# Five edits to a two-layer decoder trunk: RWKV's logistic functions on ScalarE, the skip load, the order of the rotary tables, the norms' sums and one buffer

## The chip, the cores and the metric

The kernel runs on one core of one Trainium2 chip, in one launch. The metric is the device time of a run in microseconds (us), and what is compared is the median of several runs. All times inside a run are counted from the start of its profiled span.

## The reference

Two consecutive layers of a hybrid decoder trunk are computed for one sequence of 512 tokens, model width 1024, everything in float32. Cut to the parts that the change touches:

```python
def even_mixer(h, ...):                      # layer 0
    proj = rms_norm(h, norm) @ w_in
    y_mla = mla_group(...)                   # 8 heads, rotary positions, causal softmax
    y_rw = rwkv7_group(...)                  # 8 heads of 64
    return jnp.concatenate([y_mla, y_rw], axis=-1) @ w_out

def rwkv7_group(p, ...):
    w_log = -jax.nn.softplus(-(w0 + jnp.tanh(xw) @ w2)) - 0.5
    decay = jnp.exp(-jnp.exp(w_log.astype(jnp.float32)))
    a = jax.nn.sigmoid(a0 + xa @ a2)
    ...
    y = wkv7_scan(r_h, heads(decay), k_h, v_h, -kk, kk * a_h)
    ...

def mamba2_mixer(h, ...):                    # layer 1
    ...
    y = ssd_chunked(xf * dt[..., None], dt * A, b_in, c_in)
    y = y + xf * d_skip.astype(jnp.float32)[:, None]
    ...
```

The decay is exp of a constant times the logistic function of its argument, so each pair of heads needs two logistic functions of 128x512 elements: one for the decay, one for `a`. After each mixer come a cross-attention into 256 memory tokens and a SwiGLU feed-forward, each behind its own RMS norm and added into the residual.

## The kernel before, in words

Activations lie transposed: the residual `hT` is eight tiles of 128 features by 512 tokens. Every large product is made in three matmuls on reduced-precision halves. An operand is split into a high part (`whi`, `xh`: a copy with rounding on ScalarE, L122) and a low part (`wlo`, `xl`: the remainder, on VectorE or GpSimd, L136 and L139), and TensorE adds high by high, low by high and high by low into one PSUM bank named `lin` (all matmuls on L117). Weights arrive as blocks `wraw` of 128x1024 floats (512 KB) in two buffers (L175), requested by SyncE's queue; `lo_turns` says which engine makes the next `wlo`. A block's buffer is asked for again as soon as both halves of the block before have been made.

Stages, in us: first norm and projection 0 to 60; RWKV and MLA, interleaved, 60 to 460; cross-attention 0 from 465 to 555; feed-forward 0 to 914; the Mamba mixer to 1353; cross-attention 1 to 1426; feed-forward 1 to the end. A scheduler turns the written order into one list per engine, by its own simulation of times; each engine then works through its list in order, and waits where an operand is late. Around RWKV the written order comes from a `Dense` queue of projection pieces that `weave` mixes with the steps of RWKV's head pairs (`front`, `within`, `across`) and with MLA's pairs.

What the change touches:

- `prenorm` (L337 to L368) splits `hT` into `xh` and `xl` and sums the squares of the eight tiles into `ss`. Squares 0 to 2 (0 to 3 in the first norm) are made on GpSimd, the others on ScalarE. Additions below `DVA` (5; 6 in the first norm) are GpSimd's, the others VectorE's. `fin` puts one matmul with ones on `ss` (`preno_pr`) and two activations that make the reciprocal root `R`. There are six such norms; `SQA, DVA, PX` stand on L180.
- In the first norm each finished `lin` bank is scaled by `R` into a `pd` tile on VectorE before the bank can be filled again.
- `mla_setup` (L1222) makes the rotary tables: positions, range reduction (`rope`, `angk`, `nrk`: some twenty operations on VectorE) and sines on ScalarE. It is called on L814 behind the last operation in `switch`; the Mamba layer's small loads (`odpar`, `dcol`) are issued beside it from ScalarE's queue (L816 to L820). `dcol` holds the skip factor of the Mamba heads and is first read at about 1006 us (L139, `y<-xf,dcol,odd_m_py`).
- `front` (L936) begins a head pair. It calls `sigmoid` (L931) on the tiles `fa` (decay) and `av` (a): an exponential on ScalarE, then an addition of 1 (L933) and a reciprocal (L934) on VectorE. The running sum of `fa` (L952, `fb`) and two exponentials of it (`E`, `fc`) follow. There are four pairs, so eight such functions.
- `steps` (L1510) makes the Mamba step sizes. The exponentials `ecum` of the running sums (`cum`) take the buffer `z0`, and two DMAs carry them to DRAM; the gate `z` uses the same buffer next.

Of the kernel before, what the change touches and what calls it, by code (L numbers as in the profile page):

```python
# [10 lines left out]
F32 = mybir.dt.float32  # L11
# [4 lines left out]
ALU = mybir.AluOpType  # L16
# [63 lines left out]
def kernel(ctx: ExitStack, tc: tile.TileContext, a: dict, out: bass.AP, stage: str = "exfoXF"):  # L80
# [64 lines left out]
    def cst(k):  # L145
        o, n = _COFF[k]
        return ctab[:, o:o + n]

    ident = cst("ident")
    bones = cst("bones")  # L150
    invf = cst("invf")
    ones = cp.tile([P, P], F32, name="ones")
    V.memset(ones, 1.0)
# [25 lines left out]
    held = []  # L179
    SQA, DVA, PX = (3, 5, 3)  # L180
    HOLDK = 3
# [155 lines left out]
    def prenorm(xp, gains, tmp=("ss", "sq", 2), tag="ps", before=lambda k: None):  # L337
# [3 lines left out]
        tss, tsq, bufs = tmp  # L341
        ss = xp.tile([P, T], F32, tag=tss, name=nm("ss"))
        for k in range(KD):
            before(k)
# [6 lines left out]
            xl.append(l_)  # L351
            if k == 0:
                tt(G, ss, hT[k], hT[k], ALU.mult)
            else:
                sq = xp.tile([P, T], F32, tag=tsq, name=nm("sq"), bufs=bufs)
                if k < (4 if gains is evc else SQA):
                    tt(G, sq, hT[k], hT[k], ALU.mult)
                else:
                    act(sq, hT[k], AF.Square)
                tt(G if k < (6 if gains is evc else DVA) else V, ss, ss, sq, ALU.add)  # L360

# [378 lines left out]
    def even_mixer():  # L740
# [6 lines left out]
        with pool("rwkv", side="right") as rp, pool("mlac", side="right") as cp_, pool("rwdram", space=DRAM) as dp:  # L747
# [15 lines left out]
            with psum(lin=4, ps=2):  # L763
# [49 lines left out]
                turn_rows(rows, False)  # L813
                with tc.issue_after(switch[-1].ins):  # L814
                    mla_setup(ml, xp, rt)
                    nc.scalar.dma_start(odpar[96:128, 0:1], a["ssm_dt_bias"][0].rearrange("(p o) -> p o", o=1))  # L816
                    nc.scalar.dma_start(odpar[96:128, 1:2], a["ssm_a_log"][0].rearrange("(p o) -> p o", o=1))
                    dsrc = a["ssm_d"][0].rearrange("(i j) -> j i", j=2)
                    for j in range(2):
                        nc.scalar.dma_start(dcol[j * 64:(j + 1) * 64, :], dsrc[j].partition_broadcast(64))  # L820
                logs()
# [86 lines left out]
    def rwkv_steps(rp, rt, rw, loaded):  # L908
# [21 lines left out]

        def sigmoid(o, x, negb):  # L931
            act(o, x, AF.Exp, scale=-1.0, bias=negb)
            V.tensor_scalar(o, o, 1.0, None, op0=ALU.add)  # L933
            V.reciprocal(o, o)  # L934

# [544 lines left out]
    def odd_mixer():  # L1480
# [11 lines left out]
        with pool("odd") as op, pool("oddram", space=DRAM) as dp, \  # L1492
# [17 lines left out]
            def steps(o):  # L1510
# [17 lines left out]
                nc.sync.dma_start(cdram, cum[q, :])  # L1528
                ecum = i_("z0")
                act(ecum[q, :], cum[q, :], AF.Exp)  # L1530
# [280 lines left out]
```

## Time and profile before

| what | value |
|---|---|
| median of three runs | 1801.33 us (1799.94 to 1806.09) |
| profiled execution: its own time | 1798.9 us |
| profiled execution: span of the trace | 1797.1 us |
| mean granted TensorE clock | 0.981 |
| TensorE busy | 1733.4 us (96%) |
| VectorE busy | 1087.6 us (61%) |
| ScalarE busy | 742.9 us (41%) |
| GpSimd busy | 232.8 us (13%) |
| chain that ended last | PE 86%, DVE 6%, DMA 3%, ACT 3% |

PE is TensorE, DVE VectorE, ACT ScalarE, POOL GpSimd, SP SyncE; L12 is line 12 of the kernel printed above. A row of a timeline gives the start and the duration of an instruction (or of a run of equal ones, x7) and, in brackets, how long its engine sat idle before it and what ended that. [...] Matmuls are pipelined, so a busy TensorE is not one at its peak.

### The profile page before, as it was taken

What the parts mean: (1) busy time and instruction counts of PE and PEld (TensorE: products, weight loads), DVE (VectorE), ACT (ScalarE), POOL (GpSimd) and SP (SyncE); (2) the same over time, 40 slices, a digit from 0 to 9 for tenths busy, and PEclk for the clock granted to TensorE, in tenths of its full rate; (3) what the DMA queues carried; (4) which work ended last, traced back from release to release, by engine and by line L of the source; (5) the groups of instructions that cost most, each with busy time, mean ns of one, the idle gap of its engine ahead of it and who ended that gap; (6) DMA issues with size and microseconds to landing.
All of it is one profiled execution on the core that took longest, in us unless ns stands there. A gap on an engine that the chain in (4) does not pass through costs nothing.

```text
span 1797.1 us, 25503 instructions
## 1 busy us (share of the span) xinstructions
PE 1733.4 (96%) x10192; PEld 1379.4 (77%) x10192; DVE 1087.6 (61%) x1707; ACT 742.9 (41%) x1273; POOL 232.8 (13%) x204
## 2 busy tenths in 40 slices
PE   7899999999899999999998999999999999999998
PEld 5667767777677888888876777777887788888886
DVE  6585687758566434343467779787776844443533
ACT  3443455455344213222345555454545532222222
POOL 6222211212312000101020010100020200000000
PEclk9999999999899999999998999999999999999999
DMA  5232100012213333333333433333232133333232
GB/s 160 71 92 85 49 20 25 26 60 75 79 38 92 94 99 95 100 94 101 99 91 110 112 95 115 103 118 99 91 117 71 52 102 94 94 105 95 94 97 92
DMA packets 171869, 157.15 MB, mean 87 GB/s; under 512 B 12075, under 2 KB 150182, under 8 KB 171750
## 3 DMA queue, kind: packets, MB, share of 16 engines
q1 hardware_dynamic: 169574, 155.51, 28.8%
q8 instruction: 80, 1.31, 0.3%
q14 instruction: 39, 0.32, 0.1%
q10 hardware_dynamic: 2176, 0.01, 0.1%
HBM read 150.90 MB, written 4.59 MB: 87 GB/s over the span
## 4 chain that ended last, share of the span: by engine, by line
PE 86%; DVE 6%; DMA 3%; ACT 3%; issue 1%; SPq 1%; ACTq 0%; DVEq 0%
PE lin L117 67%; PE xattn_q L117 2%; PE odd_m_py L117 2%; PE rw_x L117 1%; PE mla_sc L117 1%; DMA wraw<-in_ev_w_in_dram 1%; DVE xl L139 1%; PE rw_gram L117 1%; PE mla_q L117 1%; PE mla_pv L117 1%; PE mla_kv L117 1%; PE rw_y L117 1%; DVE wlo L136 1%; PE xattn_po L117 1%; PE mla_pT L1447 1%
## 5 line engine op out<-in xcount | busy, mean ns | idle before, releaser
L122 ACT ACTIVATE whi<-wraw 128x1024 fp32r<-128x1024 f32 (+1 forms) x255 | 266.2, 1044 | 615.1 <-PE lin L117 555.5
L136 DVE TENSOR_TENSOR wlo<-wraw,whi 128x1024 fp32r<-128x1024 f32 (+2 forms) x219 | 270.1, 1233 | 355.3 <-ACT whi L122 352.3
L117 PE MATMUL lin<-xh,whi 128*128 128x512 f32 x1192 | 475.0, 401 | 8.6 <-ACT whi L122 4.8
L117 PE MATMUL lin<-xl,whi 128*128 128x512 f32 x1192 | 470.6, 395 | 1.4 <-DVE xl L139 1.4
L117 PE MATMUL lin<-xh,wlo 128*128 128x512 f32 x1192 | 452.8, 395 | 1.1 <-DVE wlo L136 0.9
L117 PEld LDWEIGHTS lin<-xh,whi 128*128 128x128 f32 x1192 | 225.5, 189 | 62.2 <-ACT whi L122 6.4
L117 PEld LDWEIGHTS lin<-xl,whi 128*128 128x128 f32 x1192 | 225.4, 189 | 52.9 <-DVE xl L139 2.7
L117 PEld LDWEIGHTS lin<-xh,wlo 128*128 128x128 f32 x1192 | 224.7, 189 | 52.8 <-DVE wlo L136 2.0
L136 DVE TENSOR_TENSOR hT<-hT,lin 128x512 f32<-128x512 f32 x160 | 108.0, 685 | 83.9 <-PE lin L117 83.3
L136 POOL TENSOR_TENSOR wlo<-wraw,whi 128x1024 fp32r<-128x1024 f32 (+1 forms) x36 | 85.8, 2382 | 452.4 <-ACT whi L122 452.4
L117 PE MATMUL lin<-gl,whi 128*128 128x512 f32 x352 | 137.2, 390 | 0.5 <-DVE gl L136 0.5
L117 PE MATMUL lin<-gh,whi 128*128 128x512 f32 x352 | 136.1, 390 | 0.0
L117 PE MATMUL lin<-gh,wlo 128*128 128x512 f32 x352 | 125.6, 389 | 0.0
L136 DVE TENSOR_TENSOR s<-lin,R 128x512 f32<-128x512 f32 x88 | 60.1, 690 | 52.3 <-PE lin L117 52.3
L117 PEld LDWEIGHTS lin<-gl,whi 128*128 128x128 f32 x352 | 66.1, 188 | 14.4 <-DVE gl L136 0.9
L117 PEld LDWEIGHTS lin<-gh,wlo 128*128 128x128 f32 x352 | 66.1, 188 | 13.7
L117 PEld LDWEIGHTS lin<-gh,whi 128*128 128x128 f32 x352 | 66.0, 188 | 13.6
L122 ACT ACTIVATE s<-s 128x512 f32<-128x512 f32 x44 | 27.4, 623 | 69.0 <-DVE s L136 69.0
L117 PE MATMUL lin<-oyh,whi 128*128 128x512 f32 x128 | 51.8, 405 | 1.2 <-ACT oyh L122 1.2
L122 ACT ACTIVATE seg<-cumB,tms 128x128 f32<-128x128 f32 x128 | 40.1, 390 | 29.1 <-PE odd_m_py L117 24.6
L117 PE MATMUL lin<-oyl,whi 128*128 128x512 f32 x128 | 51.4, 402 | 0.4 <-DVE oyl L139 0.4
L117 PE MATMUL lin<-oyh,wlo 128*128 128x512 f32 x128 | 51.4, 402 | 0.0
(439 smaller groups left out, 2742.2 us busy)
## 6 DMA issues: line engine op xcount, KB each, us to landing
wraw<-in_ffn_w_dram SPq DMA_DIRECT2D x176, 256.0 KB
wraw<-in_ffn_w_dram SPq DMA_DIRECT2D x44, 512.0 KB
wraw<-in_od_w_in_dram SPq DMA_DIRECT2D x41, 512.0 KB
wraw<-in_ev_w_in_dram SPq DMA_DIRECT2D x17, 512.0 KB
wraw<-in_xa_wkv_dram SPq DMA_DIRECT2D x16, 512.0 KB
cumB<-cdram SPq DMA_DIRECT2D x16, 512.0 KB
wraw<-in_od_w_out_dram SPq DMA_DIRECT2D x16, 512.0 KB
wraw<-in_ev_w_out_dram SPq DMA_DIRECT2D x8, 512.0 KB
```

Source lines behind the costliest of these rows:

```text
L117: last_mm[0] = TE.matmul(o, l, r, start=start, stop=stop, **kw)
L122: ins = S.activation(o, i, f, scale=scale, bias=bias, **kw)
L136: return e.tensor_tensor(o, x, y, op=op)
L139: return V.scalar_tensor_tensor(o, x, sc, y, op0=op0, op1=op1)
L1447: TE.transpose(pt[:, kt * P:(kt + 1) * P], pr_[:, kt * P:(kt + 1) * P], ident)
```

## The change

Five edits:

1. `sigmoid`: the addition and the reciprocal on VectorE become a logarithm of (1 + x) and an exponential of its negative on ScalarE.
2. The skip load: two DMAs into `dcol` that step over every other element become one DMA of the whole row of 32 numbers to all partitions (`dall`), from which GpSimd copies the odd and even columns.
3. Table order: `mla_setup` and the small loads are kept, on the engine of the norm's last addition, behind that addition (`summed`).
4. Norm sums: `DVA` goes from 5 to 3, and in the five later norms the squares and additions from number 3 on are written behind all eight splits.
5. `ecum` takes the buffer `oyh3` in place of `z0`.

```diff
-    SQA, DVA, PX = (3, 5, 3)
+    SQA, DVA, PX = (3, 3, 3)
...
+        first = gains is evc
+
+        def squares(k):
+            if k == 0:
+                tt(G, ss, hT[k], hT[k], ALU.mult)
+                return
+            sq = xp.tile([P, T], F32, tag=tsq, name=nm("sq"), bufs=bufs)
+            if k < (4 if first else SQA):
+                tt(G, sq, hT[k], hT[k], ALU.mult)
+            else:
+                act(sq, hT[k], AF.Square)
+            summed[:] = [tt(G if k < (6 if first else DVA) else V, ss, ss, sq, ALU.add)]
+
         for k in range(KD):
...
-            if k == 0:
-                tt(G, ss, hT[k], hT[k], ALU.mult)
-            else:
-                sq = xp.tile([P, T], F32, tag=tsq, name=nm("sq"), bufs=bufs)
-                if k < (4 if gains is evc else SQA):
-                    tt(G, sq, hT[k], hT[k], ALU.mult)
-                else:
-                    act(sq, hT[k], AF.Square)
-                tt(G if k < (6 if gains is evc else DVA) else V, ss, ss, sq, ALU.add)
+            if first or k < DVA:
+                squares(k)
+        for k in range(DVA, 0 if first else KD):
+            squares(k)
...
-                with tc.issue_after(switch[-1].ins):
+                with tc.issue_after(switch[-1].ins), tc.issue_after(summed[0].ins):
                     mla_setup(ml, xp, rt)
...
-                    dsrc = a["ssm_d"][0].rearrange("(i j) -> j i", j=2)
+                    dall = xp.tile([P, 16, 2], F32, name="dall")
+                    nc.scalar.dma_start(dall.rearrange("p i j -> p (i j)"), a["ssm_d"][0].partition_broadcast(P))
                     for j in range(2):
-                        nc.scalar.dma_start(dcol[j * 64:(j + 1) * 64, :], dsrc[j].partition_broadcast(64))
+                        G.tensor_copy(dcol[j * 64:(j + 1) * 64, :], dall[j * 64:(j + 1) * 64, :, j])
...
         def sigmoid(o, x, negb):
+
             act(o, x, AF.Exp, scale=-1.0, bias=negb)
-            V.tensor_scalar(o, o, 1.0, None, op0=ALU.add)
-            V.reciprocal(o, o)
+            act(o, o, AF.Ln, bias=1.0)
+            act(o, o, AF.Exp, scale=-1.0)
...
-                ecum = i_("z0")
+                ecum = i_("oyh3")
```

How the lists of instructions move is shown at three places. The first is VectorE in the first norm, before; `xl` ends the splits, `rope`, `nrk` and `angk` are table work, `ss` the sum, `colt` the gains, `pd` the first scaled projections:

```order
L139 SCALAR_TENSOR_TENSOR angk_476<-nrk_477,angk_476 128x64
L1238 TENSOR_SCALAR angk_476<-angk_476 128x64
L136 TENSOR_TENSOR ss_174<-ss_174,sq_261 128x512
L136 TENSOR_TENSOR ss_174<-ss_174,sq_274 128x512
L276 COPY colt<-ps_445 128x64
L276 COPY colt<-ps_448 128x128
L1541 TENSOR_SCALAR colt<-colt 128x24
L1542 TENSOR_SCALAR colt<-colt 128x96
L136 TENSOR_TENSOR pd_401<-lin_285,R_173 128x512
L136 TENSOR_TENSOR pd_411<-lin_286,R_173 128x512
```

And with the change, from the last split on (line numbers are up to 13 higher there):

```order
L139 SCALAR_TENSOR_TENSOR xl_271<-hT_83,evc,xh_270 128x512
L277 COPY colt<-ps_329 128x64
L909 TENSOR_SCALAR one_mu<-colt 128x14
L910 TENSOR_SCALAR one_ka<-colt 128x4
L911 TENSOR_SCALAR colt<-colt 128x8
L912 TENSOR_SCALAR nkk_c<-colt 128x4
L136 TENSOR_TENSOR ss_174<-ss_174,sq_261 128x512
L136 TENSOR_TENSOR ss_174<-ss_174,sq_274 128x512
L1257 CAST rope_453<-rope_451 128x512
L1262 MEMSET trig_141 64x512
```

The two additions have moved ahead of all table work. Twenty rows of table and gain work, beginning with the last two above, now stand between them and the first `pd`.

The second place is ScalarE at the first head pair, before (`whi_691` is the high half of the weight block that TensorE takes next; `fb` is the running sum from VectorE):

```order
L122 ACTIVATE vs_508<-pd_612,one_mu 128x512
L122 ACTIVATE fa_629<-rw_w_627,colt 128x512
L122 ACTIVATE whi_691<-wraw_651 128x1024
L122 ACTIVATE fa_674<-ks_507,colt 128x512
L122 ACTIVATE E_704<-fb_672 128x8x64
L122 ACTIVATE fc_707<-fb_672 128x512
L122 ACTIVATE av_635<-rw_a_633,colt 128x512
L122 ACTIVATE sst_687<-pd_684,one_mu 128x512
L122 ACTIVATE whi_742<-wraw_695 128x1024
```

With the change:

```order
L122 ACTIVATE vs_510<-pd_614,one_mu 128x512
L122 ACTIVATE fa_631<-rw_w_629,colt 128x512
L122 ACTIVATE fa_631<-fa_631 128x512 x2
L122 ACTIVATE fa_676<-ks_509,colt 128x512
L122 ACTIVATE E_706<-fb_674 128x8x64
L122 ACTIVATE fc_709<-fb_674 128x512
L122 ACTIVATE whi_693<-wraw_653 128x1024
L122 ACTIVATE av_637<-rw_a_635,colt 128x512
L122 ACTIVATE av_637<-av_637 128x512
L122 ACTIVATE sst_689<-pd_686,one_mu 128x512
L122 ACTIVATE av_637<-av_637 128x512
L122 ACTIVATE whi_744<-wraw_697 128x1024
```

The logarithm and the second exponential stand there as the two rows more on `fa` and on `av`, with no table load between them, and the weight split has gone behind `fa`, `E` and `fc`. A little ahead of this, ScalarE's two DMAs of `dcol` (64x16x1 each) have become one of `dall` (128x32).

The third place is VectorE in the norm of cross-attention 0, before, from the seventh low half on:

```order
L139 SCALAR_TENSOR_TENSOR xl_5281<-hT_83,colt,xh_5280 128x512
L136 TENSOR_TENSOR wlo_5297<-wraw_5294,whi_5296 128x1024
L139 SCALAR_TENSOR_TENSOR xl_5274<-hT_82,colt,xh_5273 128x512
L136 TENSOR_TENSOR ss_5232<-ss_5232,sq_5270 128x512
L136 TENSOR_TENSOR ss_5232<-ss_5232,sq_5277 128x512
L136 TENSOR_TENSOR ss_5232<-ss_5232,sq_5284 128x512
L136 TENSOR_TENSOR wlo_5367<-wraw_5364,whi_5366 128x1024
```

With the change:

```order
L139 SCALAR_TENSOR_TENSOR xl_5271<-hT_83,colt,xh_5270 128x512
L136 TENSOR_TENSOR wlo_5299<-wraw_5296,whi_5298 128x1024
L139 SCALAR_TENSOR_TENSOR xl_5267<-hT_82,colt,xh_5266 128x512
L136 TENSOR_TENSOR ss_5234<-ss_5234,sq_5274 128x512
L136 TENSOR_TENSOR ss_5234<-ss_5234,sq_5277 128x512
L136 TENSOR_TENSOR ss_5234<-ss_5234,sq_5280 128x512
L136 TENSOR_TENSOR ss_5234<-ss_5234,sq_5283 128x512
L136 TENSOR_TENSOR ss_5234<-ss_5234,sq_5286 128x512
L136 TENSOR_TENSOR wlo_5369<-wraw_5366,whi_5368 128x1024
```

Five additions in place of three stand behind the weight split and ahead of the next one; GpSimd's list has two additions in place of four.

## Rows read from the trace of the kernel before

**Rows 1.** Windows: length; busy PE, PEld, DVE, ACT, POOL; clock, DMA share, GB/s.

```profile
25.00:50.00 25.00, 18.83 (x67) 12.78 (x66) 18.77 (x38) 9.76 (x14) 10.62 (x6) 0.86 0.39 100
60.00:107.00 47.00, 38.45 (x166) 27.10 (x165) 31.85 (x33) 15.52 (x22) 13.33 (x11) 0.96 0.32 88
107.00:200.00 93.00, 93.00 (x912) 70.68 (x909) 59.85 (x113) 37.94 (x74) 20.43 (x26) 0.96 0.26 74
200.00:260.00 60.00, 55.91 (x735) 39.92 (x736) 48.89 (x119) 32.59 (x79) 13.38 (x12) 0.91 0.11 32
260.00:440.00 180.00, 178.62 (x2110) 133.31 (x2107) 125.16 (x319) 94.55 (x217) 30.93 (x29) 1.00 0.14 41
```

**Rows 2.** Timeline of the first norm, 26 to 47 us.

```profile
26.30 0.43 DVE L1244 CAST rope<-rope 128x512 f32<-128x512 int32 x1 [0.61 <-DMA rope<-in_positions_dram]
...
27.70 0.69 DVE L267 COPY hT<-trans_x 128x512 f32<-128x512 f32 x1
...
35.13 0.63 ACT L122 ACTIVATE sq<-hT 128x512 f32<-128x512 f32 x1 [1.99 <-POOL ss L136]
...
41.88 0.69 DVE L136 TENSOR_TENSOR ss<-ss,sq 128x512 f32<-128x512 f32 x1 [0.70 <-ACT sq L122]
...
42.72 1.80 PE L117 MATMUL preno_pr<-ss,ones 128*128 128x512 f32 x2 [4.17 <-DVE ss L136]
...
45.28 0.63 ACT L122 ACTIVATE R<-R 128x512 f32<-128x512 f32 x1
...
46.18 1.28 DVE L136 TENSOR_TENSOR pd<-lin,R 128x512 f32<-128x512 f32 x2
```

**Rows 3.** The page's DMA queues: packets, MB, share of 16 engines.

```profile
q10 hardware_dynamic: 2176, 0.01, 0.1%
```

**Rows 4.** Windows at the start of RWKV, columns as in group 1.

```profile
70.00:78.00 8.00, 8.00 (x33) 5.66 (x32) 4.75 (x3) 0.00 (x0) 0.00 (x0) 1.00 0.05 1
78.00:84.00 6.00, 1.17 (x6) 0.64 (x5) 0.22 (x1) 1.31 (x2) 0.00 (x0) 0.99 0.60 176
84.00:88.00 4.00, 3.86 (x9) 2.21 (x8) 2.96 (x3) 3.54 (x6) 1.74 (x3) 0.58 0.42 118
98.00:106.00 8.00, 4.42 (x32) 2.79 (x31) 8.00 (x7) 0.87 (x1) 6.16 (x3) 1.00 0.44 133
```

**Rows 5.** The chain that ended last, 55 to 110 us: start, us, what.

```profile
64.15 18.10 DMA wraw<-in_ev_w_in_dram
```

**Rows 6.** The tile fa: line, engine, operation, ns (least, median, most), starts.

```profile
L122 ACT ACTIVATE fa<-rw_w,colt x4: 669/690/692, 66.7 to 301.3; 128x512 f32<-128x512 f32 x4
L933 DVE TENSOR_SCALAR fa<-fa x4: 417/427/428, 69.1 to 302.0; 128x512 f32<-128x512 f32 x4
L934 DVE RECIPROCAL fa<-fa x4: 3352/3353/3353, 69.6 to 302.5; 128x512 f32<-128x512 f32 x4
```

**Rows 7.** Timeline of the norm of cross-attention 0, VectorE and GpSimd.

```profile
472.39 10.97 DVE L139 SCALAR_TENSOR_TENSOR xl<-hT,colt,xh 128x512 fp32r<-128x512 f32 x7
472.50 6.87 POOL L136 TENSOR_TENSOR ss<-ss,sq 128x512 f32<-128x512 f32 x4
...
484.42 0.74 DVE L139 SCALAR_TENSOR_TENSOR xl<-hT,colt,xh 128x512 fp32r<-128x512 f32 x1
```

**Rows 8.** Windows of the same place, columns as in group 1.

```profile
475.00:485.00 10.00, 6.03 (x21) 3.77 (x22) 10.00 (x7) 2.74 (x4) 6.56 (x4) 0.91 0.00 0
485.00:495.00 10.00, 10.00 (x32) 7.63 (x32) 3.62 (x6) 3.01 (x4) 0.00 (x0) 0.74 0.31 106
```

**Rows 9.** Timeline of the Mamba step sizes, VectorE and ScalarE, 968 to 978 us.

```profile
971.78 1.29 DVE L139 SCALAR_TENSOR_TENSOR z<-lin,R 128x512 f32<-128x512 f32 x2 [3.94 <-DMA xdram<-z]
...
973.76 1.87 ACT L122 ACTIVATE seg<-cumB,tms 128x128 f32<-128x128 f32 x6 [4.41 <-DMA cumB<-cdram]
975.53 0.61 ACT L122 ACTIVATE th<-Ct 128x512 f32<-128x512 f32 x1
```

**Rows 10.** Groups of instructions on ScalarE: count, busy us, mean ns of one.

```profile
L122 ACT ACT_TABLE_LOAD x12 | 15.4, 1283 | 0.2
```

More of the change, by code (lines that the diff above doesn't have):

```diff
@@ L151 @@
     invf = cst("invf")
+    summed = []
     ones = cp.tile([P, P], F32, name="ones")
```

## The prediction

> **What bounds the kernel now.** I read the windows by stage first, because the share of busy time over a whole trunk hides which stage has anything to give. TensorE is busy for all of 107 to 200 us and for 178.62 of the 180 us from 260 to 440 at the full clock, whereas it does 18.83 of 25 us around the first norm, 38.45 of 47 at the start of RWKV and 55.91 of 60 in the middle of it [rows 1]. So the changed places can only pay where TensorE stands idle, or where its granted clock is low just after an idle stretch. Then I read the timelines of those gaps, from TensorE's restart back to what released it, and last the durations of the operations that are exchanged. The sum is made against the profiled run, 1798.9 us (span 1797.1); the median of the three runs, 1801.3, lies 2.4 above it, and I add that at the end. About 0.3%, 5.4 us, is what a measurement of this kernel can tell from no change.
>
> **Table order (first norm).** TensorE waits 4.17 us for the second DVE addition into `ss`, which runs at 41.88. VectorE spends the time before on rope table rows; the last square but one was ready at 35.13 + 0.63 = 35.8 [rows 2]. After the change the additions stand ahead of the rope rows. Then: addition 35.8 to 36.5, the last square on ScalarE (0.63) to 37.1, addition to 37.8. TensorE's own matmuls last to 42.72 − 4.17 = 38.55, so it no longer waits, and `R`, which was done at 45.28 + 0.63 = 45.91, 3.19 after the norm's matmul began, can be done at 41.7. But twenty rope and table rows now stand on VectorE between the additions and the first `pd`. The only price in the rows is the five from 26.30 to 27.70: 0.28 us each, so 5.6 us, from 37.8 to 43.4. The first `pd` starts there instead of at 46.18, and TensorE's `lin`, which needs the PSUM banks that `pd` empties, restarts with it: **−2.8 us**. Bounds: if the rows slip into gaps, `R` decides and it is −4.4; if they stretch as badly beside GpSimd as some do now, 0.
>
> **Skip load.** Two DMAs on the ACT queue, issued before ScalarE reaches the first sigmoid, carry `dcol` one element at a time: 2 × 64 × 16 = 2,048 of queue q10's 2,176 packets [rows 3]. From 70 to 78 us DMA engines are 5% busy and move 1 GB/s [rows 4], and the weight block requested at 64.15 needs 18.10 us to land [rows 5]. [...] With one request of 128 contiguous pieces the block can land about 13 us sooner: 512 KB at the 118 GB/s of the 84 to 88 row is 4.4 us. The split on ScalarE, now behind two more activations, is then still ready before TensorE needs it near 79, so the idle 4.8 us and 4 × 0.42 = 1.7 us of clock go: **−6.5 us**. The two GpSimd copies of 16 columns run beside a GpSimd that is busy 13.33 of 47 us [rows 1]; they wait for a small load, and if it were late the weight split behind them would be too. I take 0 for them, 1 us at most.
>
> [...] No run yet shows the load without its element-wise form.
>
> **Sigmoids.** Eight times, VectorE loses an addition and a reciprocal, 0.42 + 3.35 us [rows 6], 30.2 us in all. ScalarE gains two activations; the nearest row is the first exponential, 0.69 us [rows 6], so 16 × 0.69 = 11 us. Only where VectorE is on TensorE's path does this pay.
> In the first pair (60 to 107) it is: from 98 to 106 VectorE is busy all 8 us and TensorE 4.42 [rows 4]. The reciprocal of `av` alone, 3.35 with its 0.42, is as long as that gap of 3.6: **−3.6 us**, bounds 0 (the stretched operations beside GpSimd remain) and −3.6.
> In the other three pairs (107 to 440) VectorE loses 22.6 of 59.85 + 48.89 + 125.16 = 233.9 busy us out of 333, and ScalarE gains 8.3 on 165 [rows 1]. TensorE's idle there sums to 4.1 + 1.4 = 5.5 us, its lost clock to 93 × 0.04 + 60 × 0.09 = 9.1 [rows 1]. So 14.6 us is the most that can come, and most of it lies in one piece, 200 to 260, where VectorE is busy 81% of the time. I take **−3 us**: half the idle. Bounds −14.6, and on the other side the new dependent chain on ScalarE, priced as the slower rival below.
>
> **Norm sums.** In cross 0, seven `xl` take 10.97 us, 1.57 each, beside GpSimd's four `ss` additions (6.87 us) and its following weight split; the eighth, alone, takes 0.74. The weight split that TensorE needs stands between the seventh and the eighth [rows 7]. TensorE is idle 3.97 us of 475 to 485, then is granted 0.74 for 10 us [rows 8]. Two additions fewer free 3.4 us of contention, in which two `xl` at 1.57 become two at 0.74: 1.7 us. With as much again from a shorter idle stretch's clock (2.6 us are lost there now) I take **−3 us**, bounds 0 and −6.6. The two additional additions on VectorE (0.7 each) stand behind the split that TensorE waits for, and before the next one, and are hidden by the matmuls of 485 to 495, TensorE busy 10 of 10. The other four norms, without such a gap, get 0.
>
> **Exponentials' buffer.** VectorE's `z` at 971.78 waits 3.94 us until the DMA that reads the exponentials has ended, because both use `z0`. That wait goes. But ScalarE waits 4.41 us for `cumB`, until 973.76, and the activation that the next operations on VectorE need stands behind it at 975.53 [rows 9]. What is late next is that `cumB` load, so **0**, bounds −1.4 and +0.5.
>
> **Sum.** −2.8 − 6.5 − 3.6 − 3 − 3 = −18.9 on 1798.9 gives 1780.0; with 2.4 for the median 1782.4. I say **1782**.
>
> **The rivals.**
> *Smaller gain (0.22).* Only the DMA gap goes. The rope rows stretch beside GpSimd and hold `pd`; VectorE's relief is hidden since TensorE is busy anyway in 107 to 200; the `xl` still run beside a GpSimd split. −6.5: **1795**. For it: TensorE is 93 of 93 busy. Against it: the 98 to 106 row.
> *The gap is not the skip load's (0.08).* The weight block is late for another reason; −12.4 is left: **1789**. For it: the two streams are on different queues. Against it: the engines stand nearly idle while the block is due, so it is not held up by other bytes.
> *Larger gain (0.18).* All of the 14.6 us in 107 to 440 come back, since VectorE's buffers are free earlier: −30.5, **1771**.
> *Slower: new bubbles in RWKV (0.06).* Three dependent activations stand in ScalarE's line ahead of the weight split and of attention's `pr`; each short hole in TensorE's stream also costs clock. The stretch 200 to 260 shows what that is like: 4.1 idle and 5.4 of clock in 60 us [rows 1]. All 333 us like that are 9.5 × 5.55 = 53, against 14.6 now: +38, less the 15.9 of the other terms: **1823**. It decides from 21 us of new bubbles on. For it: the order of everything in 107 to 440 shifts. Against it: ScalarE is only half busy there.
> *It does not do what it says (0.02).* If the logarithm and the exponential lay in different tables, each sigmoid would load twice at 1.28 us [rows 10]: 16 × 1.28 = 20.5 us more on ScalarE, and three activations are then over 4 us, as long as what they replace. The instruction order shows no added load, so the time is the smaller gain's, **1795**, at worst.
>
> The forecast itself has the remaining 0.44.
>
> **How the numbers follow.** Faster by over 0.3% means below about 1796. The forecast, the larger gain and the other-cause case lie there, and somewhat over half of the smaller gain: 0.44 + 0.18 + 0.08 + 0.12 = 0.82. Same: the rest of the smaller gain and of the last case, 0.12. Slower: 0.06. The range runs from 1766, a little below the larger gain because the first norm and cross 0 may reach their own bounds, to 1798, a little above the smaller one.
>
> **What would show it.** Right: the packets of the ACT queue fall from 2,176 to a few hundred, and no idle stretch of TensorE is left at 79 to 84; the norm's matmul begins by 39 us and the first `pd` at about 43; from 98 to 106 TensorE is busy 7 us or more; in cross 0 the seven `xl` take under 9.5 us; the seg activation still waits for `cumB`. Wrong: a weight block still landing 15 us late; `pd` at 46; in 107 to 440 more than 6 us idle or a clock under 0.95; a table load beside a sigmoid.

## The result, and the profile after

The changed kernel takes 1777.6 us (median of four runs, 1777.1 to 1778.4) against 1801.7 in the runs beside it; the ratio is 0.9864, 95% interval 0.9848 to 0.9879. That is 24 us shorter where 19 were forecast, and inside the range. The profiled run took 1777.7 us, its span is 1775.9 and its mean clock 0.984.

Where it came from shows in the windows by stage, with the columns of [rows 1] and [rows 4] (the clock is the share of full speed that TensorE was granted, the DMA share the part of the time that the DMA engines were busy):

```profile
25.00:50.00 25.00, 19.59 (x72) 14.31 (x71) 21.13 (x43) 10.20 (x15) 11.11 (x8) 0.86 0.41 106
60.00:107.00 47.00, 45.24 (x207) 33.90 (x206) 32.51 (x58) 24.32 (x39) 13.42 (x14) 0.96 0.38 105
107.00:200.00 93.00, 90.98 (x995) 69.50 (x995) 56.21 (x122) 42.39 (x87) 22.72 (x28) 1.00 0.25 73
200.00:260.00 60.00, 58.11 (x782) 41.28 (x772) 39.62 (x116) 34.08 (x82) 9.10 (x10) 0.89 0.05 15
260.00:440.00 180.00, 177.14 (x2038) 134.08 (x2035) 115.82 (x292) 96.97 (x219) 32.52 (x29) 0.99 0.16 48
...
78.00:84.00 6.00, 6.00 (x26) 4.52 (x25) 1.37 (x3) 2.36 (x4) 1.23 (x2) 1.00 0.46 131
84.00:88.00 4.00, 4.00 (x19) 3.22 (x18) 3.97 (x5) 1.26 (x2) 1.20 (x1) 1.00 0.30 80
98.00:106.00 8.00, 8.00 (x42) 6.47 (x39) 7.08 (x20) 3.71 (x7) 0.73 (x1) 1.00 0.41 107
```

The stretch 60 to 107 has 45.24 us of TensorE work in place of 38.45. The hole at 78 to 84, the low clock behind it (0.58 in 84 to 88, now 1.00) and the hole at 98 to 106 are all filled. What is missing in 60 to 107 is a wait of 1.8 us for `pd` behind the first `rw_w`, from 65.1 to 66.9, and a low clock after it; before there was neither. The windows 66 to 70 us, before and after:

```profile
66.00:70.00 4.00, 4.00 (x17) 3.06 (x17) 3.07 (x4) 1.38 (x3) 2.71 (x2) 1.00 0.05 0
66.00:70.00 4.00, 3.14 (x8) 2.52 (x9) 3.06 (x4) 2.56 (x4) 2.57 (x3) 0.57 0.55 139
```

The same rows show the weight block: requested at 65.5 us, it is through by 70, where it needed 18.10 us before [rows 5]. The first norm, 25 to 50, has hardly more work than before. One of the signs that the forecast named for being wrong did appear: in 107 to 440 TensorE is idle for 6.8 us (5.5 before), and from 200 to 260 its clock is 0.89 (0.91 before). These windows hold other work than before; from the first `rw_x` to the first `xattn_q`, the same work in both, the idle time is 7.6 us in place of 8.5.

The queue that carried the single elements, from the page's part on DMA queues, answers to [rows 3]:

```profile
q10 hardware_dynamic: 240, 0.02, 0.0%
```

The first norm, as a timeline (start, duration, engine) and answering to [rows 2]:

```profile
36.92 0.69 DVE L136 TENSOR_TENSOR ss<-ss,sq 128x512 f32<-128x512 f32 x1 [0.70 <-ACT sq L122]
...
37.75 1.10 PE L117 MATMUL preno_pr<-ss,ones 128*128 128x512 f32 x2
...
39.29 2.57 DVE L1247 TENSOR_SCALAR rope<-rope 128x512 f32<-128x512 f32 x1
...
39.61 0.63 ACT L122 ACTIVATE R<-R 128x512 f32<-128x512 f32 x1
...
44.20 1.29 DVE L136 TENSOR_TENSOR pd<-lin,R 128x512 f32<-128x512 f32 x2
```

The norm's matmul begins 5.0 us sooner and `R` is ready at 40.24 in place of 45.91, but the first `pd` starts only 2.0 us sooner. Among the waits of TensorE up to 110 us are these two (engine, line, what for, us in total, times, longest):

```profile
PE ps L276 <- DVE colt L277: 3.6, 1, 3.6
PE lin L117 <- DVE pd L136: 3.6, 2, 1.8
```

The wait of 4.2 us for the sum has become one of 3.6 for the gains (`colt`), which VectorE copies behind the same table rows.

The norm of cross-attention 0, with its timeline answering to [rows 7] and its windows to [rows 8]:

```profile
458.17 6.79 DVE L139 SCALAR_TENSOR_TENSOR xl<-hT,colt,xh 128x512 fp32r<-128x512 f32 x7
458.28 3.47 POOL L136 TENSOR_TENSOR ss<-ss,sq 128x512 f32<-128x512 f32 x2
466.01 2.88 DVE L139 SCALAR_TENSOR_TENSOR xl<-hT,colt,xh 128x512 fp32r<-128x512 f32 x1
```

```profile
465.00:475.00 10.00, 9.55 (x39) 6.78 (x37) 8.48 (x8) 3.73 (x5) 2.39 (x1) 1.00 0.34 105
475.00:485.00 10.00, 9.22 (x50) 7.58 (x48) 2.69 (x7) 4.03 (x7) 2.36 (x1) 1.00 0.18 52
```

Seven `xl` take 6.79 us in place of 10.97, and the clock stays at 1.00. The eighth is now the slow one, 2.88 against 0.74, beside GpSimd's weight split (465.95 us, 2.39 long). TensorE waits 0.2 us at most for a low half there, and its wait for the weight split `wlo` has gone from 3.6 us to 0.3.

In the Mamba step sizes ScalarE still waits, as in [rows 9]:

```profile
952.83 1.86 ACT L122 ACTIVATE seg<-cumB,tms 128x128 f32<-128x128 f32 x6 [4.94 <-DMA cumB<-cdram]
954.59 0.61 ACT L122 ACTIVATE th<-Ct 128x512 f32<-128x512 f32 x1
```

Windows at fixed times hold other work once everything stands earlier, so the places are better told apart by the time between the starts of the same matmuls. In us, from the timelines of before and after: up to the first `rw_w` 65.2 and 64.0; on to the first `rw_x` 57.7 and 49.8; to the first `rw_y` on `S` 74.3 and 71.0; to the first `xattn_q` 274.3 and 272.6; to the first `lin` on `oh` 52.6 and 46.3; to the first transpose of the output 1247.0 and 1246.8. So, between these two traces, 8 us lie in the first head pair, 5 in the rest of RWKV, 6 in cross-attention 0, 1 in the first norm, and nothing behind. Not all of it is the change's: up to `xattn_q` each of these stretches also differs, by 2 to 3 us, between traces of kernels that were not changed there.

### The profile page after: what moved, and what is told of

Same layout as the page of the kernel before. It is cut to its first block, busy times and chain, and to the rows that moved or that the text cites. A ratio compares the mean times of both kernels' runs of the same rounds, so it can differ in the third digit from the quotient of the medians.

```text
span 1775.9 us, 25504 instructions
## 1 busy us (share of the span) xinstructions
PE 1726.1 (97%) x10192; PEld 1375.8 (77%) x10192; DVE 1053.9 (59%) x1701; ACT 752.5 (42%) x1289; POOL 212.0 (12%) x196
## 4 chain that ended last, share of the span: by engine, by line
PE 89%; DVE 4%; ACT 3%; DMA 2%; issue 1%; SPq 1%; ACTq 0%
PE lin L117 69%; PE xattn_q L117 2%; PE odd_m_py L117 2%; PE rw_x L117 2%; PE mla_sc L117 1%; PE rw_gram L117 1%; PE mla_q L117 1%; PE mla_pv L117 1%; PE mla_kv L117 1%; PE rw_y L117 1%; PE xattn_po L117 1%; ACT whi L122 1%; PE odd_m_pS L117 1%; PE odd_m_ps L117 1%; PE mla_pT L1460 1%
## 5 line engine op out<-in xcount | busy, mean ns | idle before, releaser
L117 PEld LDWEIGHTS lin<-xl,whi 128*128 128x128 f32 x1192 | 225.7, 189 | 52.5 <-issue 2.5
L117 PEld LDWEIGHTS lin<-xh,wlo 128*128 128x128 f32 x1192 | 225.0, 189 | 51.6 <-issue 1.9
L117 PE MATMUL lin<-oyh,whi 128*128 128x512 f32 x128 | 51.8, 405 | 1.2 <-ACT oyh L122 1.2
```

The lines of the kernel that those rows point to most:

```text
L117: last_mm[0] = TE.matmul(o, l, r, start=start, stop=stop, **kw)
```

## The experiments

Twelve kernels were run. "Ratio" is to the kernel before, timed beside them on the same chip; its medians there were 1804 to 1804.8 us, and single runs went from 1799.9 to 1808.7. A difference of 2 us in total is therefore no evidence; the stretches of the traces tell more.

**One part of the change at a time.** Each of these is the kernel before with one of the five edits.

*The skip load alone.*

```diff
-                    dsrc = a["ssm_d"][0].rearrange("(i j) -> j i", j=2)
+                    dall = xp.tile([P, 16, 2], F32, name="dall")
+                    nc.scalar.dma_start(dall.rearrange("p i j -> p (i j)"), a["ssm_d"][0].partition_broadcast(P))
                     for j in range(2):
-                        nc.scalar.dma_start(dcol[j * 64:(j + 1) * 64, :], dsrc[j].partition_broadcast(64))
+                        G.tensor_copy(dcol[j * 64:(j + 1) * 64, :], dall[j * 64:(j + 1) * 64, :, j])
```

> The kernel before with the skip load alone changed. Theory (the 2,048 single-element pieces hold the weight block up): the block requested at 64 us lands within 5 us, TensorE has no idle stretch at 79 to 84, the first kk matmul comes 6 to 7 us earlier, and the run is 6.5 us shorter (ratio 0.9964). [...] Second rival (the gap only moves): idle at 79 goes, but a wait of several us for the reciprocals appears before 107 and the gain is under 3 us.

Measured: 1797.3 us, ratio 0.9961 (0.9946 to 0.9976), 7 us. Its windows:

```profile
78.00:84.00 6.00, 6.00 (x26) 4.52 (x25) 5.87 (x3) 1.74 (x3) 3.00 (x2) 1.00 0.33 87
84.00:88.00 4.00, 4.00 (x19) 3.23 (x18) 2.06 (x4) 1.91 (x4) 0.10 (x1) 1.00 0.65 180
88.00:98.00 10.00, 8.48 (x51) 6.18 (x49) 9.97 (x10) 2.79 (x4) 6.51 (x3) 1.00 0.43 136
98.00:106.00 8.00, 6.66 (x28) 4.66 (x29) 7.63 (x18) 2.35 (x5) 0.93 (x3) 0.79 0.43 137
```

The hole of [rows 4] at 78 to 84 is gone; the one for VectorE's chain (2.6 us for `rw_bonus`) stays, and has moved ahead to the end of 88 to 98. The theory holds; that the gap only moves does not.

*The logistic functions alone.*

```diff
-            V.tensor_scalar(o, o, 1.0, None, op0=ALU.add)
-            V.reciprocal(o, o)
+            act(o, o, AF.Ln, bias=1.0)
+            act(o, o, AF.Exp, scale=-1.0)
```

> The kernel before with the logistic functions alone moved to ScalarE. Theory (they are worth something by themselves): the gap at 79 to 84 stays, the stretch 98 to 106 is full again (3.6 us) and 107 to 440 gives the 5 us that it gave in the whole change: 8 us shorter (ratio 0.9955). Rival (the reciprocals are hidden by the weight gap and only count once it is gone): at most 3 us shorter. Rival with the other sign (ScalarE becomes the one waited for): slower.

Measured: 1793.4 us, ratio 0.9945 (0.9928 to 0.9962), 10 us. Two of its windows:

```profile
78.00:84.00 6.00, 0.25 (x2) 0.00 (x0) 0.54 (x1) 1.62 (x2) 0.00 (x0) 0.74 0.60 176
98.00:106.00 8.00, 8.00 (x58) 5.81 (x57) 6.86 (x13) 2.46 (x4) 3.25 (x3) 1.00 0.45 144
```

TensorE still runs dry at 78 to 84, but 98 to 106 is full. So the reciprocals cost time by themselves, weight gap or not. With ScalarE doing three activations in place of one, TensorE's longest new wait is the one of 5.8 us for `av` in that same hole, where it waited for weights before. It is the weight gap still: `av` stands behind a weight split on ScalarE's list, and that split waits for its block.

```profile
82.38 1.06 ACT L122 ACTIVATE whi<-wraw 128x1024 fp32r<-128x1024 f32 x1 [10.46 <-DMA wraw<-in_ev_w_in_dram]
```

*The norm sums alone* (the squares and `DVA` as in the diff of the change).

> The kernel before with the norm sums alone changed. Theory (contention of VectorE with GpSimd in cross-attention 0): seven xl take 6.8 us in place of 11.0, the wait of 3.6 us for the weight split goes, and the whole run is 6.3 us shorter (ratio 0.9965), the amount by which cross-attention 0 moved in the whole change. Rival, the forecast's own figure: 3 us, the rest of cross-attention 0 having come from what ran before it.

Measured: 1797.5 us, ratio 0.9962 (0.9949 to 0.9975), 6.9 us: the theory. The seven `xl` take 6.79 us here as well, and TensorE's wait for the weight split goes from 3.6 us to 0.3.

*The table order alone* (`mla_setup` behind `summed`).

> The kernel before with the table order alone changed. Theory: the sum is ready 5 us earlier, but the rows that now stand ahead of the first pd take 6.5 us, so the first pd starts 2 us earlier and the run is 1.5 to 2 us shorter (ratio 0.999). Rival (what is ready earlier is given back before 65 us): no difference. The forecast's figure: 2.8 us.

Measured: 1803.3 us, ratio 1.0002 (0.9990 to 1.0013). Its timeline:

```profile
38.58 1.10 PE L117 MATMUL preno_pr<-ss,ones 128*128 128x512 f32 x2 [1.49 <-DVE ss L136]
...
45.26 1.28 DVE L136 TENSOR_TENSOR pd<-lin,R 128x512 f32<-128x512 f32 x2
...
67.94 0.61 PE L117 MATMUL lin<-xh,whi 128*128 128x512 f32 x1 [1.54 <-DVE pd L136]
```

The matmul is 4.1 us sooner, `pd` 0.9, the time the same: the rival. What is ready earlier is given back. The first `rw_w` starts at 65.3 us (65.2 before), and behind it stands a wait of 1.5 us for a `pd` that the kernel before does not have, with a clock of 0.72 from 66 to 72. The changed kernel has the same wait, 1.8 us.

*The exponentials' buffer alone.*

```diff
-                ecum = i_("z0")
+                ecum = i_("oyh3")
```

> The kernel before with the buffer of the exponentials alone changed. Forecast's step: VectorE's wait of 3.9 us for z goes, ScalarE still waits 4 to 5 us for cumB with the activation of Ct behind it, and the time does not move by more than 1 us (ratio 0.9995 to 1.0005). Rival (the wait mattered): 2 us or more shorter.

Measured: 1804.7 us, ratio 1.0006 (0.9994 to 1.0017): nothing, as forecast. In its trace `z` no longer waits, and ScalarE does:

```profile
977.52 1.86 ACT L122 ACTIVATE seg<-cumB,tms 128x128 f32<-128x128 f32 x6 [4.75 <-DMA cumB<-cdram]
```

The stretches of these five traces, and of some that follow, in us:

| kernel | rw_w to rw_x | rw_x to rw_y | rw_y to xattn_q | xattn_q to lin on oh |
|---|---|---|---|---|
| before | 57.7 | 74.3 | 274.3 | 52.6 |
| skip load alone | 51.6 | 74.4 | 275.0 | 51.5 |
| logistic functions alone | 54.3 | 73.9 | 272.0 | 51.8 |
| norm sums alone | 61.0 | 74.4 | 275.5 | 45.2 |
| table order alone | 61.7 | 73.1 | 276.5 | 51.6 |
| buffer alone | 59.5 | 71.5 | 276.9 | 52.5 |
| change without logistic functions | 51.9 | 71.7 | 275.3 | 47.6 |
| the change | 49.8 | 71.0 | 272.6 | 46.3 |

Each edit moves its own stretch. The logistic functions give 3 us from `rw_y` to `xattn_q` (272.0 and 272.6 with them, 274.3 to 276.9 without) and 3 to 7 in the first pair while the hole is there, 2 once it is gone. The stretch from `rw_x` to `rw_y`, 71 or 74, follows no edit.

The first stretch scatters as well: it is 57.7 in the trace of before and 59.5 to 61.0 in others that leave it alone. The clock behind the hole for VectorE's chain makes the difference. The windows 107 to 112 us of the kernel before, and of the one with only the order in the norms changed (it follows below):

```profile
107.00:112.00 5.00, 5.00 (x28) 4.02 (x25) 4.66 (x12) 3.05 (x7) 0.75 (x1) 1.00 0.64 201
```

```profile
107.00:112.00 5.00, 5.00 (x17) 2.89 (x16) 4.51 (x10) 1.24 (x2) 0.84 (x2) 0.50 0.72 211
```

Six traces of kernels keep both holes. In this window that of before shows 1.00, those of the buffer alone and of the constant alone (below) 0.66, and that of the order alone 0.50. Those of the norm sums alone and of the table order alone show 0.82 and 0.91 over 106 to 125 us, where that of before has 1.00, as has that of the logistic functions alone. So in five of the six that hole costs some 2 to 3 us of clock besides its idle time (an estimate: each window times what its clock lacks, 1.7 to 3.4 us), and the trace from which the forecast was made did not show it.

The ratios of the five, 0.9961, 0.9945, 0.9962, 1.0002 and 1.0006, leave 0.9876 when their differences are added up, against 0.9864 (0.9848 to 0.9879) for the whole: within these intervals the edits add up, and nothing shows that one needs another.

**The logistic functions taken out of the change.**

```diff
-            act(o, o, AF.Ln, bias=1.0)
-            act(o, o, AF.Exp, scale=-1.0)
+            V.tensor_scalar(o, o, 1.0, None, op0=ALU.add)
+            V.reciprocal(o, o)
```

> The changed kernel with the logistic functions put back to VectorE. Theory (the edits add up): it loses what the logistic functions gave alone, 10 us, to about 1787.5 (ratio to the kernel before 0.991). Rival (with the weight gap gone the reciprocals are exposed more): over 13 us lost. Rival (with the gap gone VectorE has room): under 6 us lost.

Measured: 1787.9 us (1781.8 to 1797.1), ratio 0.9921 (0.9889 to 0.9953). By the medians 10.2 us are lost, what they gave alone. But the six runs lie in two groups, 1781.8 to 1784.5 (mean granted clock 0.987 to 0.988) and 1791.2 to 1797.1 (0.979 to 0.983), and the median falls between them, where no run is. The rivals' ends are not excluded, and that the theory's 1787.5 was met is in part luck.

**What in the norm sums pays.** One kernel has only the constant, the other only the order.

```diff
-    SQA, DVA, PX = (3, 5, 3)
+    SQA, DVA, PX = (3, 3, 3)
```

> The kernel before with two of GpSimd's four additions of each later norm given to VectorE (the constant DVA from 5 to 3), the order in which the norm is written left alone. Theory (GpSimd's additions beside the seven xl are what costs): nearly the whole 6.8 us of the norm sums, the seven xl under 8 us. Rival (VectorE's own additions, now written between the splits, stand ahead of the weight split): the additions take the place of the stretch and under 3 us are gained.

Measured: 1797.3 us, ratio 0.9964 (0.9954 to 0.9974).

```diff
         for k in range(KD):
...
+            if first or k < DVA:
+                squares(k)
+        for k in range(DVA, 0 if first else KD):
+            squares(k)
```

> The kernel before with the order alone changed: squares and additions from number 5 on are written behind all eight splits, GpSimd keeps its four additions. Theory (contention): no gain, the seven xl still take about 11 us. Rival (the order of the squares on ScalarE and of the weight split is what pays): over 3 us.

Measured: 1804.4 us, ratio 1.0004 (0.9993 to 1.0015). The timeline of VectorE at this norm, first of the constant alone, then of the order alone:

```profile
475.57 6.79 DVE L139 SCALAR_TENSOR_TENSOR xl<-hT,colt,xh 128x512 fp32r<-128x512 f32 x7
482.27 1.21 DVE L136 TENSOR_TENSOR wlo<-wraw,whi 128x1024 fp32r<-128x1024 f32 x1
483.41 2.88 DVE L139 SCALAR_TENSOR_TENSOR xl<-hT,colt,xh 128x512 fp32r<-128x512 f32 x1
```

```profile
477.40 10.97 DVE L139 SCALAR_TENSOR_TENSOR xl<-hT,colt,xh 128x512 fp32r<-128x512 f32 x7
```

All of it is in the two additions taken from GpSimd; the scheduler had found the later order by itself.

**Why the weight block was late.** First the dose: the same loads once more, into a scratch tile.

```diff
                     for j in range(2):
                         nc.scalar.dma_start(dcol[j * 64:(j + 1) * 64, :], dsrc[j].partition_broadcast(64))
+                    dmore = xp.tile([P, 16], F32, name="dmore")
+                    for j in range(2):
+                        nc.scalar.dma_start(dmore[j * 64:(j + 1) * 64, :], dsrc[j].partition_broadcast(64))
+                    G.tensor_copy(dmore[:, 0:1], dmore[:, 1:2])
```

> The kernel before with two more element-wise loads of the same numbers, into a scratch tile that nothing of the result reads, behind the two of dcol: 4,096 single-element pieces in place of 2,048. Theory (the weight block waits until the pieces are through, at some 106 pieces per us): the next weight block lands some 19 us later, near 101 us in place of 82, TensorE is idle for about 24 us in place of 4.8 and the run is about 20 us longer, near 1822. [...]

Measured: 1821.4 us (two runs), ratio 1.0098 (1.0067 to 1.0129), 17 us longer. The queue's packets go from 2,176 to 4,256. ScalarE's second request for the scratch tile, SyncE's request for the weight block, ScalarE's wait for it, and the window between, with the columns of [rows 1]:

```profile
64.05 9.65 ACTq L823 DMA_DIRECT2D dmore<-in_ssm_d_dram  x1
...
77.37 0.38 SPq L175 DMA_DIRECT2D wraw<-in_ev_w_in_dram  x1
...
103.07 1.06 ACT L122 ACTIVATE whi<-wraw 128x1024 fp32r<-128x1024 f32 x1 [23.13 <-DMA wraw<-in_ev_w_in_dram]
```

```profile
77.00:96.00 19.00, 8.92 (x28) 6.08 (x28) 7.96 (x8) 2.30 (x4) 0.00 (x0) 0.77 0.05 0
```

The block is there for ScalarE at 103.1 in place of 82.7, 20 us later, as the theory has it, but only in part for its reason. It was also requested 13 us later, at 77.4 in place of 64.15: ScalarE sat for 12.7 us while it issued the second pair of loads, and the splits that free the buffer came late. The rest bears the theory out. With the block requested nothing but elements moved from 77 to 96 us (0 GB/s); the last elements landed at 100.4, 36.3 us after their request; and the block was there 2.7 us behind them, some 25 us after its own request, where it had needed 18. The 17 us of the whole run are not clean evidence either, because the scratch copy also held GpSimd's list for 41 us, and TensorE waited 15.4 us for a `pd` behind it. The same elements as before, from another queue:

```diff
-                        nc.scalar.dma_start(dcol[j * 64:(j + 1) * 64, :], dsrc[j].partition_broadcast(64))
+                        nc.gpsimd.dma_start(dcol[j * 64:(j + 1) * 64, :], dsrc[j].partition_broadcast(64))
```

> The kernel before with the two element-wise loads of dcol issued from GpSimd's queue in place of ScalarE's, still 2,048 single elements. Theory A (what is held up is making the pieces of both hardware-issued queues, since the engines that carry them stand 95% idle): the weight block at 64 us lands within 5 us, no idle stretch at 79 to 84, about 6.5 us shorter, unless GpSimd itself is late for its pd and weight splits while it makes the pieces. Theory B (the DMA engines take the small pieces one after the other whatever queue they come from): the idle stretch stays as before, within 3 us of its time.

Measured: 1818.0 us, ratio 1.0070 (1.0047 to 1.0093), 13 to 14 us longer, which neither theory named. On GpSimd nothing orders these loads behind the norm, and the scheduler put them at 1.4 us, ahead of the input. They do as much harm there. The queue's row, the window 10 to 20 us of the kernel before, and the windows 0 to 20 us of this one:

```profile
q0 software_dynamic: 64, 0.01, 1.0%
```

```profile
10.00:20.00 10.00, 10.00 (x47) 8.31 (x46) 7.48 (x5) 5.15 (x7) 9.76 (x7) 1.00 0.68 234
```

```profile
0.00:10.00 10.00, 2.14 (x9) 1.74 (x9) 2.05 (x11) 1.88 (x2) 3.91 (x12) 1.00 1.06 65
10.00:20.00 10.00, 0.00 (x0) 0.00 (x0) 0.00 (x0) 0.00 (x0) 0.00 (x0) 1.00 1.17 90
```

TensorE does nothing from 10 to 20 us, where it did 10 us of work before, because the input is late: the DMA engines moved 65 and 90 GB/s in these two windows, where the kernel before has 248 and 234. The first `rw_w` comes 19 us later, and 6 of these are regained when no gap follows at 79. Here the profile books the elements as 1.0% of 16 engines' span, 18 us of every engine, but DMA shares of 1.06 and 1.17 mean that these bookings overlap with other transfers, which still moved 65 and 90 GB/s. On queue q10 the same elements were booked as 0.1%, 1.8 us of an engine, while everything else stood at 1 GB/s. Some 18 to 20 us for the same 2,048 elements from either queue (on q10 requested at 58.1 and 58.8 us, with 0 to 3 GB/s moved from 62 to 78; on q0 landed 14.3 and 25.2 us after their requests, 19.8 in the middle) fits theory B, that the elements take the DMA engines' time and other transfers wait. But the two hold-ups differ in kind, and what an engine does in that time no row shows. Nor does one show how the pieces are made, on which theory A rests; GpSimd was through with its two requests at 3.3 us, after 1.90 us. Shown is that the elements hold other transfers up, and that moving them to another queue only moves the harm; which part of the way they block is not shown.

**Two waits that were left.** The rotary tables go behind the second `pd`:

```diff
-                with tc.issue_after(switch[-1].ins), tc.issue_after(summed[0].ins):
+                with tc.issue_after(switch[-1].ins), tc.issue_after(scaled[1].ins):
...
-                        tt(V, pd[:, 1:T + 1], o, R, ALU.mult)
+                        scaled.append(tt(V, pd[:, 1:T + 1], o, R, ALU.mult))
```

> The changed kernel with the rotary tables and small loads held behind the second pd in place of behind the norm's last addition. Theory (the twenty rows ahead of the first pd give the earlier sum back): the first pd starts near 40.5 us, when R is ready, in place of 44.2, TensorE no longer waits 3.6 us for colt and 1.8 for pd ahead of it, and the run is 3 to 4 us shorter than the changed kernel, near 1774. Rival (later tables hold up the tanh of lo and the first pair, as pd already waits 1.8 us at 60 to 65): what is gained at 45 is lost by 66 and the time is the changed kernel's, 1777.6.

Measured: 1774.5 us (1769.3 to 1777.2), ratio 0.9825 (0.9800 to 0.9850). In its timeline:

```profile
40.93 1.28 DVE L136 TENSOR_TENSOR pd<-lin,R 128x512 f32<-128x512 f32 x2
```

The first `pd` starts 3.3 us sooner than in the changed kernel, the wait for `colt` falls from 3.6 to 0.3, and the first `rw_w` is 3.8 us sooner: what the table order was worth, once the rows stand behind `pd` too. By the first `rw_x` it is 5.9 us ahead, since the wait for `pd` behind `rw_w` is 0.9 us here and the clock stays at 1.00. The next stretch, to `rw_y`, takes 73.9 us against 71.0, and eats half of that (the last section has that stretch). By times alone this kernel is not set apart from the changed one; the intervals touch.

Then `seg` behind the tanh of the first `Ct` as well:

```diff
-                act(th, half, AF.Tanh)
+                gated[:] = [act(th, half, AF.Tanh)]
...
+            last_c = gated[0]
...
                         for c in range(NC):
+                          with tc.issue_after(last_c.ins):
                             act(sg[:, c, :], cB[:, c * P:(c + 1) * P], AF.Relu, scale=-1.0, bias=tms[:, 1, c, h:h + 1])
```

> The kernel of b1_pd1 with the seg activations of the Mamba mixer also held behind the tanh of the first Ct. Theory (that tanh stands behind a wait of 4.9 us for cumB, and TensorE waits 5.3 us for Ct): TensorE restarts 5 us earlier, at full clock, and the mixer ends 4 to 6 us earlier, so 1768 to 1770. Rival (seg itself, which waits for cumB, is what the next matmuls need): under 1.5 us.

Measured: 1772.8 us (1770.7 to 1777.5), ratio 0.9827 (0.9809 to 0.9846). This interval lies clear of the changed kernel's, if only just; it is no lower than that of the kernel one step before. In its timeline of ScalarE the tanh runs before the wait:

```profile
946.76 0.63 ACT L122 ACTIVATE th<-Ct 128x512 f32<-128x512 f32 x1 [0.46 <-DVE Ct L139]
950.74 2.44 ACT L122 ACTIVATE seg<-cumB,tms 128x128 f32<-128x128 f32 x8 [3.34 <-DMA cumB<-cdram]
```

From the first transposes of `Bt` to the first `odd_m_ps` it takes 14.9 us where the kernel one step before took 18.6: 3.7 us, a little under the 4 to 6 expected, since TensorE then waits 2.2 us for `xdt`. The medians of the two kernels, 1.8 us apart, do not tell them apart; the trace does.

## Why the prediction was right, point by point

- **Skip load** (forecast −6.5, alone −7.0). Right in size and place. Both parts of its sum, 6 − 1.17 us of idle and 4 × (1 − 0.58) us of clock [rows 4], are gone in the changed kernel, whose windows there have 6.00 of 6 and 1.00. One inference of the prediction does not stand, though: it took the share of 0.05 in [rows 4] for engines standing nearly idle, and argued with it against the block's being held up by other bytes. The share counts what the profile books, and it books the same 2,048 elements as 1.8 us of an engine on queue q10 and as 18 us on q0. Whether the engines stood idle is open. On q0, where the profile counts 64 packets, other traffic still moves at 65 to 90 GB/s beside the elements. On q10, where it counts 2,176, everything together moved at 1 GB/s from 70 to 78 us with a block requested on another queue (q1). The block was held up, and it no longer is once the elements are gone. Why, no run shows.
- **Logistic functions** (forecast −3.6 and −3, alone −9.9, taken out again 10.2). The second term, for the other three pairs, came out as said: 3 us from `rw_y` to `xattn_q`. The first pair's 98 to 106 went from 4.42 to 8.00 us of work, but alone the edit gives 3 to 7 us from `rw_w` to `rw_x`, so that term was undersized where the hole is still there: it counted one idle stretch and none of the clock behind it, some 2 to 3 us in five of the six traces that keep the hole. With the weight gap gone it is 2. What the medians say beyond these stretches, up to 5 us when the functions are taken out of the change, was not found: the profiled run of that kernel, 1784.5 us, belongs to the shorter of its two groups and was itself only 6.8 longer than the change's, and none of the longer runs left a trace. ScalarE did not become the bound; it is busy 42.39 us of 93.
- **Norm sums** (forecast −3, alone −6.9). The mechanism was right, and the term "two `xl` at 1.57 become two at 0.74" mis-sized: the seven together lost 4.2 us, not 1.7. With two additions fewer GpSimd was through before its weight split, and the split, which used to run beside the seven `xl`, now runs beside the eighth. With the wait for the split, 3.6 us, all of its clock came back too, 0.91 and 0.74 to 1.00, not half of it.
- **Table order** (forecast −2.8, alone nothing; −1.2 at `rw_w` within the change). The failed step is the price of the twenty rows and what stands among them. From the end of the additions to `pd` VectorE took 6.6 us, not 5.6, with one `rope` row stretched to 2.57, from 0.43 before, beside GpSimd's split (38.80 us, 2.77 long); and the copies of `colt`, which TensorE waits for, stood in the same list. The text named `pd` as what is late next, and missed `colt`. It also took what is gained at the first `pd` as kept. But a later `pd`, behind the first `rw_w`, starts at 66.0 us (65.3 before), and there TensorE, which now comes 1.2 us sooner, waits 1.8 us and goes on at a clock of 0.57.
- **Buffer** (forecast 0, alone 1.0006). Right, with the reason given: `cumB` was late next. Moving one activation ahead of that wait is what pays there (3.7 us in the last experiment).
- **Base.** The profiled run of before, 1798.9 us, lies at the low end of its runs: larger sets have their median at 1804. Setting the sum of −18.9 against it, with 2.4 for the median, started some 3 us too low, and the undersized terms (3 us of the logistic functions, 4 of the norm sums, less the 3 of the table order that did not come) made up for it. So the mechanisms of the skip load, the logistic functions and the norm sums were right, but that 1782 came within 5 us of the measured time is in part luck: a base and three terms were each off by 3 to 4 us, not all the same way.

Of the rivals, "only the DMA gap goes" falls with the second and third experiment, "not the skip load's" with the first. The larger gain did not come either: from the first `rw_x` to the first `xattn_q` 5 us were gained, not 14.6, and 3 of them are the scatter of the last section. Nor did table loads beside the logistic functions: ScalarE makes 19 in all before and after. Of the slower rival there is no sign: in that stretch TensorE was idle for 8.5 us before and is for 7.6 now. Nor does each short hole cost clock, as that rival has it: behind the one at 98 to 106 the trace of before shows 1.00 from 107 to 112.

## What to carry to other kernels

Look for small strided loads that are in flight just before a weight block is late: here 8 KB in pieces of one element held up a block of 512 KB by some 13 us (18.10 us to landing, under 5 without them), and from another queue they held up the input. Before an operation is moved ahead on a list, go through what it is moved ahead of and who waits for each of those; the table order gained 5 us at one instruction and gave them back at those that follow it. Where VectorE's operations run beside GpSimd's (here seven `xl` took 10.97 us beside four additions and the weight split, 6.79 beside two additions), count the overlap of both lists, not only the operation that is taken away.

## What was not expected of the hardware

The same instructions take 71 or 74 us. From the first `rw_x` to the first `rw_y`, the windows of the kernel before, of the one with only the buffer changed (whose lists are those of before up to the Mamba stage), and of the changed one:

```profile
122.95:197.27 74.32, 74.32 (x791) 56.16 (x792) 43.19 (x69) 26.62 (x52) 17.26 (x24) 0.95 0.24 73
```

```profile
126.62:198.08 71.46, 71.46 (x792) 54.00 (x792) 43.18 (x69) 26.65 (x52) 17.22 (x24) 1.00 0.26 75
```

```profile
113.74:184.73 70.99, 70.99 (x795) 53.78 (x796) 37.28 (x65) 28.43 (x56) 16.17 (x24) 1.00 0.26 76
```

TensorE is busy throughout in all three, and the granted clock is 0.95 or 1.00. The difference lies in one place, some 26 us into the stretch, behind a few us of small matmuls (`mla_n`, `rw_akv`, `rw_x`): there the kernel before was granted 0.50 for about 6 us, and the one with the buffer changed 1.00 for the same instructions.

```profile
149.00:152.00 3.00, 3.00 (x26) 2.07 (x25) 0.69 (x4) 0.76 (x4) 0.10 (x1) 0.50 0.56 133
```

```profile
152.67:155.67 3.00, 3.00 (x42) 2.31 (x41) 1.91 (x5) 1.68 (x5) 0.10 (x1) 1.00 0.54 122
```

So 3 of the 5 us that the rest of RWKV seems to have gained between the two profiles are not the change's. What decides between the two was not tried. The kernel before scatters by 9 us in all (1799.9 to 1808.7), the changed one by 1.3 in its four runs, the last two kernels by 7 to 8, and the change without its logistic functions by 15.
